# Sixteen experts on one core: conditional rounds for crowded experts replaced by a fixed ninth pass and one conditional block

## The chip, the cores and the metric

The kernel runs on one core of a Trainium2 chip. Its time is the device time of one execution in microseconds (us), and a kernel is told by the median of its runs. The whole network is one program in float32: TensorE multiplies matrices, VectorE and ScalarE do the elementwise work, GpSimd (POOL in the profile) some of it too, and SyncE (SP) issues the loads of weights from HBM into SBUF.

## What is computed

The network has two blocks of two layers each on 256 tokens of 1024 features. The change concerns the second block's feed-forward part, a grouped mixture of experts, which stands in both of its layers:

```python
def grouped_moe(h, router_w, router_b, w_gate, w_up, w_down):
    t = h.reshape(B * S, Dm)                                  # 256 x 1024
    logits = t @ router_w + router_b                          # 16 experts, 4 groups
    probs = softmax(logits)
    group_score = sum of the two best probs of each group
    sel_group = argmax(group_score)
    masked = where(in_group, logits, -inf)
    top_val, top_idx = top_k(masked, 2)
    top_w = softmax(top_val)
    combine = sum(one_hot(top_idx) * top_w)
    for e in range(16):
        hidden = silu(t @ w_gate[e]) * (t @ w_up[e])          # 1024 -> 512
        out = out + combine[:, e:e + 1] * (hidden @ w_down[e])  # 512 -> 1024
    return out
# around it, in each layer i of the block:
h = x * (1.0 + scale) + shift
y = grouped_moe(h, ...)
x = layer_norm_2(ALPHA * x + (1.0 + gate) * y, ln_g[i, 1], ln_b[i, 1])
```

(Cut and slightly abridged; the rest of the network is gated delta rule, dilated and differential attention, dense feed-forward layers, stick-breaking attention and retention.) Each token uses 2 of 16 experts, so an expert has 32 tokens on average, but the inputs decide how many it really has. Each expert has 6 MB of weights: 2 MB each of gate, up and down, 96 MB per layer.

## The kernel before

**Passes.** The router (`router`, up to L1876) gives each token its slot within its experts, the combine weights, and for each of 8 pairs of experts how many more than 64 tokens the fuller one has, in units of 64 (`exi`, L1869 to L1874). `moe` (from L1893) then takes the experts in pairs. Each expert of a pair has 64 slots: the first holds columns 0 to 63 of a tile, the second 64 to 127, and on TensorE their products go into rows 0 to 63 and 64 to 127 of a PSUM bank. A pass of a pair is: **gather** (L1943; VectorE writes a one-hot matrix `pe`, L1953, and TensorE multiplies x with it, L1960, so that `xs` holds the slots' tokens with features on partitions; `pt` is the way back, `cw` the weights), **gate** and **up** (L1982, 32 matmuls each), **flip** (transposes, L1989), **down** (L1996, 32 matmuls), **weigh** (L2001) and **scatter** (L2008, adds the slots to four accumulators in PSUM). The passes overlap: gather and gate of the next pair are written before down of this one, and a pair's scatter after the next gather.

**Conditional rounds.** Behind gate, up and down of each pair stands a nest of three `tc.If(vals[pr] > r)` (`extra_gate` L2016 to L2021, `extra_up` L2029 to L2031, `extra_down` L2041 to L2043). Within it the same pair is done once more for slots 64 to 127, and so on. Each branch is one on every engine, which first loads the condition into a register (L1940).

**Weights.** Pieces of 1 MB are loaded by SP in a fixed order, each into one of three rings, `wq` (8 buffers), `w` (6) and `wr` (NR = 4). `follow` asks for the loads that the pieces just used make room for, behind each branch; loads are not moved across a branch.

**The layer norm's last step.** The gathers of the first two pairs use x before the norm's scale and offset have been applied (they apply them to what they gathered); from pair 2's gather on, x itself must have them. `ln_fix` (L589 to L601) does that on GpSimd, in two halves of 512 columns: it fetches a row of scale and one of offset by DMA (L598), copies them to all partitions (L599) and multiplies and adds (L601). Its rows lie in a tile of its own, `yx`, which has one buffer and is shared with the conditional rounds' `extra_down`. What is traced in Python is scheduled by a framework: it puts instructions on their engines' queues in an order that it works out, gives tiles their buffers, and adds the waits on semaphores.

Of the kernel before, what the change touches and what calls it, by code (L numbers as in the profile page):

```python
# [21 lines left out]
P = 128  # L22
# [93 lines left out]
class Net:  # L116
# [3 lines left out]
    def __init__(self, ctx, tc, T, log=None):  # L120
# [3 lines left out]
        # the sequence of the weights' loads and splits, known from a first trace  # L124
# [3 lines left out]
        self.ltile, self.stile = {}, {}  # L128
# [24 lines left out]
    def segment(self, ny):  # L153
        """The pools of the phases with split weights: the dense ones."""
# [71 lines left out]
    def work(self, items):  # L226
        """A filler out of (ready, generator) items: always the first that is ready."""
# [51 lines left out]
    def ordered(self, *engines):  # L279
        """What is traced within stays in its order on each of these engines."""  # L280
# [13 lines left out]
    def bcast_row(self, pool, src_row, n, tag):  # L294
        """[n] of DRAM -> the same row on all partitions."""
# [7 lines left out]
    def cols(self, pool, src, n, m, tag):  # L303
        """DRAM rows src [n, m, 128] -> tile [128, m, n] (n <= 128, m * n <= 512)."""
# [19 lines left out]
    def wload(self, src, shape, ring="w"):  # L324
        """Ask for one piece of weights, up to 8 KB a partition; wtile gives it."""
# [1567 lines left out]
    def moe(self, layer, xn, out=None):  # L1893
# [11 lines left out]
        with self.wqs, tc.tile_pool(name=self.nm("wr"), bufs=NR) as self.wr, \  # L1905
# [38 lines left out]
            def gather(pr, xs=None, pt=None, cw=None, r=None):  # L1944
# [20 lines left out]
                if pt is None:  # L1965
                    return
# [223 lines left out]
```

## Time and profile before

| | us |
|---|---|
| runs | 2052.61, 2038.22, 2048.41 |
| median | 2048.41 |
| span of the profiled execution | 2037.4 |
| TensorE busy | 1817.7 (89%) |
| VectorE busy | 1052.9 (52%) |
| ScalarE busy | 710.9 (35%) |
| GpSimd busy | 294.6 (14%) |
| bytes loaded | 423.39 MB, mean 208 GB/s |

The profiled execution is told by its span alone: 2037.4 us from its first instruction to its last, 11.0 below the median of the runs and 0.8 below the fastest of them. Busy shares are means over a program of many stages, so a stage is read by itself. In the profile PE is TensorE, PEld its load of the stationary operand, DVE VectorE, ACT ScalarE, POOL GpSimd; a q behind a name means the engine's sequencer, which handles branches, register loads and semaphores. PEclk is the granted share of TensorE's full clock. The line numbers are those of the kernel before.

### The profile page before, as it was taken

The page shows a single profiled execution, that of the slowest core. Times are in us where ns is not written, and L with a number is a line of the kernel's source. Part 1 is how long each engine was busy: PE and PEld are TensorE (multiplying, and loading weights), DVE is VectorE, ACT ScalarE, POOL GpSimd, SP SyncE. Part 2 cuts the span into 40 slices and gives each one's busy share as a digit, 9 for nine tenths or more (in the row PEclk, how much of TensorE's full clock was granted, in tenths as well). Part 3 has the DMA queues.
Part 4 walks back from the last instruction along what each step waited for, and adds up shares of the span by engine and source line. Part 5 has one row for each costly group of instructions (what it writes and reads, how often), then busy time and mean ns, then how long its engine had stood idle before and what let it go on. Part 6 is the DMA issues. An engine that isn't in the chain of part 4 may idle for free. (4 is left out here: it accounts for less than half of the span.)

```text
span 2037.4 us, 29823 instructions
## 1 busy us (share of the span) xinstructions
PE 1817.7 (89%) x11817; PEld 1372.3 (67%) x11817; DVE 1052.9 (52%) x1903; ACT 710.9 (35%) x1339; POOL 294.6 (14%) x293
## 2 busy tenths in 40 slices
PE   7999998999989989999996888997789987788886
PEld 6989877999877779998884343432789864343332
DVE  5766757777567577776654121112756652111213
ACT  5334434555544455555542010110534331110101
POOL 2011104000233130004001100000424301100002
PEclk9999998999889989998997998998899998899998
DMA  8555534555764745566366997673334494899730
GB/s 252 155 166 166 187 126 164 188 186 185 219 198 135 257 157 186 187 206 194 108 217 236 343 394 286 242 269 126 127 124 147 166 370 169 327 337 361 286 141 22
DMA packets 271141, 423.39 MB, mean 208 GB/s; under 512 B 10469, under 2 KB 176951, under 8 KB 270917
## 3 DMA queue, kind: packets, MB, share of 16 engines
q1 hardware_dynamic: 266516, 415.91, 59.1%
q8 instruction: 156, 2.56, 0.5%
q0 software_dynamic: 2016, 2.49, 0.5%
q10 hardware_dynamic: 2385, 1.88, 0.3%
q14 instruction: 68, 0.56, 0.1%
HBM read 419.19 MB, written 1.05 MB: 206 GB/s over the span
## 5 line engine op out<-in xcount | busy, mean ns | idle before, releaser
L268 DVE TENSOR_TENSOR wl<-w,wh 128x1024 fp32r<-128x1024 f32 (+1 forms) x312 | 411.5, 1320 | 217.2 <-ACT wh L267 215.8
L267 ACT ACTIVATE wh<-w 128x1024 fp32r<-128x1024 f32 (+1 forms) x312 | 328.7, 1054 | 369.7 <-PE ps L394 183.9
L393 PE MATMUL ps<-xh,wh 128*128 128x256 f32 (+1 forms) x1312 | 386.6, 295 | 15.3 <-ACT xh L427 8.0
L395 PE MATMUL ps<-xh,wl 128*128 128x256 f32 (+1 forms) x1312 | 378.2, 289 | 5.2 <-DVE wl L268 5.1
L394 PE MATMUL ps<-xl,wh 128*128 128x256 f32 (+1 forms) x1312 | 378.5, 289 | 0.0
L393 PEld LDWEIGHTS ps<-xh,wh 128*128 128x128 f32 (+1 forms) x1312 | 255.7, 195 | 23.2 <-ACT xh L427 8.3
L395 PEld LDWEIGHTS ps<-xh,wl 128*128 128x128 f32 (+1 forms) x1312 | 255.1, 194 | 7.7 <-DVE wl L268 6.1
L394 PEld LDWEIGHTS ps<-xl,wh 128*128 128x128 f32 (+1 forms) x1312 | 255.8, 195 | 3.9 <-issue 1.4
L1982 PE MATMUL pc<-w,xs 128*64 128x512 f32 x512 | 153.3, 657 | 25.0 <-PEq L2043 12.4
L393 PE MATMUL ps<-wh,xh 128*128 128x256 f32 x512 | 155.8, 305 | 5.1 <-DVE rvg L264 2.0
L394 PE MATMUL ps<-wl,xh 128*128 128x256 f32 x512 | 149.0, 291 | 1.1 <-DVE wl L268 1.1
L395 PE MATMUL ps<-wh,xl 128*128 128x256 f32 x512 | 148.6, 291 | 0.2
L394 PE MATMUL pc<-wl,yh 128*128 128x512 f32 x336 | 132.7, 395 | 0.0
L393 PE MATMUL pc<-wh,yh 128*128 128x512 f32 x336 | 131.8, 396 | 0.9 <-DVE yl L268 0.9
L395 PE MATMUL pc<-wh,yl 128*128 128x512 f32 x336 | 131.3, 392 | 1.4 <-DVE yl L268 1.2
L1982 PE MATMUL ps<-w,xs 128*64 128x512 f32 x512 | 120.8, 620 | 0.0
L1982 PEld LDWEIGHTS pc<-w,xs 128*64 128x64 f32 x512 | 44.6, 148 | 109.5 <-issue 100.8
L393 PEld LDWEIGHTS ps<-wh,xh 128*128 128x128 f32 x512 | 101.3, 198 | 10.3 <-issue 2.5
L1960 PEld LDWEIGHTS ps<-pe,x 128*128 128x128 f32 x576 | 73.0, 206 | 46.5 <-issue 45.4
L394 PEld LDWEIGHTS ps<-wl,xh 128*128 128x128 f32 x512 | 101.5, 198 | 1.9 <-DVE wl L268 1.3
L395 PEld LDWEIGHTS ps<-wh,xl 128*128 128x128 f32 x512 | 100.8, 197 | 1.6 <-DVE xl L428 0.7
L1960 PE MATMUL ps<-pe,x 128*128 128x128 f32 x576 | 79.1, 296 | 21.9 <-DVE pe L1953 18.3
(538 smaller groups left out, 2734.1 us busy)
## 6 DMA issues: line engine op xcount, KB each, us to landing
w<-in_moe_w_gate_dram SPq DMA_DIRECT2D x64, 1024.0 KB, 8.7
w<-in_moe_w_up_dram SPq DMA_DIRECT2D x64, 1024.0 KB, 10.7
w<-in_moe_w_down_dram SPq DMA_DIRECT2D x64, 1024.0 KB, 8.6
w<-in_ada_w_dram SPq DMA_DIRECT2D x48, 1024.0 KB, 5.4
w<-in_ffn_w_up_dram SPq DMA_DIRECT2D x44, 1024.0 KB, 5.3
w<-in_ret_w_in_dram SPq DMA_DIRECT2D x24, 1024.0 KB, 5.3
w<-in_ffn_w_down_dram SPq DMA_DIRECT2D x22, 1024.0 KB, 4.9
w<-in_w_in_even_dram SPq DMA_DIRECT2D x21, 1024.0 KB, 5.3
```

The lines of the kernel that those rows point to most:

```text
L267: self.nc.scalar.activation(hi, src, AF.Copy)
L268: self.nc.vector.tensor_tensor(lo, src, hi.bitcast(F32), op=ALU.subtract)
L393: mm(ps, lh, rh, start=first, stop=False)
L394: mm(ps, lh, rl, start=False, stop=False)
L395: mm(ps, ll, rh, start=False, stop=last)
L1960: mm(ps[:, k * P : k * P + P], xn[:, t, (4 * a + k) * P : (4 * a + k + 1) * P], pef[:, t, :], start=t == 0, stop=t == 1)
L1982: mm(ps[64 * e : 64 * e + 64, :], xs[:, k, 64 * e : 64 * e + 64], wt[2 * (k // 4) + e][:, k % 4, :], start=k == 0, stop=k == KD - 1)
```

## The change

The conditional rounds of all pairs go, and with them their branches. In their place comes a ninth pass, `Unit(0)`, which is always done: one expert's slots beyond its first 64, 64 of them. Which expert, and from which slot on, VectorE computes behind the router (`extra_units`, new: some two dozen operations on small tiles) as a mask `m`, an offset `off` and an index `exi`. The pass gathers by mask and offset, and its six pieces of weights are loaded by SP from an address that is computed from a register (`bass.ds(unit_at(u), 1)`). Since one expert alone would fill half of TensorE's rows, its 512 hidden columns are split into two halves of 256 on the two halves of the rows, and in down its 1024 outputs likewise. What one such pass can't take is left to one conditional block, `more(1)`, nested up to the seventh unit, that stands before the last scatter.

Loads are now asked for in one sequence, without `follow`; NR goes from 4 to 6, so the rings have 20 buffers. `ln_fix`'s rows lose `yx` and take a buffer of the tag `xs`, of which there are two and which the gathers use. The last norm's rows (`gb`) move from `xs` into a buffer of the ring. Comments and docstrings were taken out throughout (not shown).

```diff
-NW, NQ, NR = 6, 8, 4
+NX = 7
+NW, NQ, NR = 6, 8, 6
...
+            if src[0] == "dynamic" and src not in self.dyn:
                 break
...
-            self.nc.sync.dma_start(v, bass.AP(tensor=self.byname[name], offset=off, ap=ap))
+            if src[0] == "dynamic":
+                src = self.dyn[src]()
+            else:
+                src = bass.AP(tensor=self.byname[src[0]], offset=src[1], ap=src[2])
+            self.nc.sync.dma_start(v, src)
...
+    def extra_units(self, mp, cnt):
+        nc = self.nc
+        E = N_EXP
+        G = nc.vector
+        tt, ts = G.tensor_tensor, G.tensor_scalar
+        io = self.moe_c[2]["iota64"]
+        tile = lambda n, *s, dt=F32: mp.tile([P, *s], dt, tag="u_" + n, name=self.nm("u" + n), bufs=1)
+        x, y, one = tile("x", E), tile("y", E), tile("one", E)
+        ts(x, cnt, 64.0, None, op0=ALU.is_gt)
+        for r in (2, 3):
+            ts(y, cnt, 64.0 * r, None, op0=ALU.is_gt)
+            tt(x, x, y, op=ALU.add)
+        c = [tile("c0", E), tile("c1", E)]
+        G.tensor_copy(c[0], x)
+        s = 1
+        while s < E:
+            G.tensor_copy(c[1][:, :s], c[0][:, :s])
+            tt(c[1][:, s:], c[0][:, s:], c[0][:, : E - s], op=ALU.add)
+            c.reverse()
+            s *= 2
+        c = c[0]
+        b = lambda v: v[:, None, :].to_broadcast([P, NX, E])
+        iu = io[:, :NX, None].to_broadcast([P, NX, E])
+        m, w = tile("m", NX, E), tile("w", NX, E)
+        tt(m, b(c), iu, op=ALU.is_gt)
+        tt(x, c, x, op=ALU.subtract)
+        tt(w, b(x), iu, op=ALU.is_le)
+        tt(m, m, w, op=ALU.mult)
+        off, ex, exi = tile("off", NX), tile("ex", NX + 1), tile("exi", NX + 1, dt=I32)
+        tt(w, m, b(x), op=ALU.mult)
+        nc.vector.tensor_reduce(off, w, axis=AX.X, op=ALU.add)
+        tt(off, off, io[:, :NX], op=ALU.subtract)
+        ts(off, off, 64.0, -64.0, op0=ALU.mult, op1=ALU.add)
+        tt(w, m, b(io[:, :E]), op=ALU.mult)
+        nc.vector.tensor_reduce(ex[:, :NX], w, axis=AX.X, op=ALU.add)
+        G.tensor_copy(ex[:, NX:], c[:, E - 1 :])
+        G.tensor_copy(exi, ex)
+        return m, off, exi
...
+            def part(u, m, a):
+                d, n = dram[m], (512, 512, 256)[m]
+                v = d[bass.ds(unit_at(u), 1), a * n : a * n + n, :]
+                return v.rearrange("o (k p) f -> p (o k) f", p=P)
...
+                if pr < NP:
+                    src = w[2 * pr + e][:, a * step : a * step + step, :]
+                else:
+                    src = ("dynamic", layer, m, a)
+                    self.dyn[src] = lambda: part(0, m, a)
...
-            slot, comb, exi = self.router(mp, hT)
+            slot, comb, cnt = self.router(mp, hT)
...
-            vals = [nc.values_load(exi[:1, pr : pr + 1], min_val=0, max_val=3) for pr in range(NP)]
...
+            def unit_at(u):
+                if u not in extra:
+                    extra[u] = nc.values_load(extra["exi"][:1, u : u + 1], engines=[mybir.EngineType.SP],
+                                              min_val=0, max_val=N_EXP - 1)
+                return extra[u]
...
+            class Unit(Pair):
...
+                    s.u = u
+                    s.wt = wt or (lambda m: [self.wtile(i) for i in pieces[NP, m]])
+                def slots(s):
+                    m, off = extra["m"], extra["off"]
+                    w = big("uw", [P, 2, NT, N_EXP])
+                    so, cb = big("uso", [P, NT, 2]), big("ucb", [P, NT, 2])
+                    b = m[:, s.u : s.u + 1, :].to_broadcast([P, NT, N_EXP])
+                    tt(w[:, 0], slot, b, op=ALU.mult)
+                    tt(w[:, 1], comb, b, op=ALU.mult)
+                    for i, o in enumerate((so, cb)):
+                        nc.vector.tensor_reduce(o[:, :, 0], w[:, i], axis=AX.X, op=ALU.add)
+                    ts(so[:, :, 0], so[:, :, 0], off[:, s.u : s.u + 1], None, op0=ALU.add)
+                    for o in (so, cb):
+                        nc.vector.tensor_copy(o[:, :, 1], o[:, :, 0])
+                    return gather(so, cb)
+                def up(s, m, xs, ps):
+                    wt = s.wt(m)
+                    for k in range(KD):
+                        for e in range(2):
+                            mm(ps[64 * e : 64 * e + 64, :256], xs[:, k, 64 * e : 64 * e + 64],
+                               wt[k // 4][:, k % 4, 256 * e : 256 * e + 256], start=k == 0, stop=k == KD - 1)
+                    return ps[:, :256]
+                def down(s, hT, cw):
+                    wt = s.wt(2)
+                    y = big("yu", [P, 2, 512], F32R)
+                    ps = self.cb("x")
+                    for f in range(4):
+                        for e in range(2):
+                            c = (f % 2) * P + 64 * (f // 2)
+                            mm(ps[64 * e : 64 * e + 64, :], hT[:, c : c + 64],
+                               wt[f // 2][:, f % 2, e * 512 : e * 512 + 512], start=f == 0, stop=f == 3)
+                    weigh(y, ps, cw)
+                    return y
+                def scatter(s, pt, y, last=False):
+                    for t in range(NT):
+                        for hf in range(2):
+                            sl = slice(64 * hf, 64 * hf + 64)
+                            for v in range(2):
+                                i = mm(acc[t][hf], pt[sl, t * P : t * P + P], y[sl, v, :],
+                                       start=False, stop=last and v == 1)
+                                tc.keep_in_program_order(i)
...
+            def more(u):
+                with tc.If(extra["n"] > u):
+                    wt = {}
+                    for m in range(3):
+                        wt[m] = []
+                        for a in range(2):
+                            k = (4, 4, 2)[m]
+                            if ("w", m, a) not in shared:
+                                ring = self.wr if m < 2 else self.wq
+                                shared["w", m, a] = ring.tile([P, 2048], F32, tag="w", name=self.nm("wx"))
+                            v = shared["w", m, a].rearrange("p (a b) -> p a b", a=k)
+                            nc.sync.dma_start(v, part(u, m, a))
+                            wt[m].append(v)
+                    it = Unit(u, wt.get)
+                    xs, pt, cw = it.slots()
+                    h = gate(it, xs, self.bank())
+                    tt(h, h, it.up(1, xs, self.bank()), op=ALU.mult)
+                    it.scatter(pt, it.down(flip(h), cw))
+                    if u < NX - 1:
+                        more(u + 1)
...
+            its = [Pair(pr) for pr in range(NP)] + [Unit(0)]
+            cur = its[0].slots()
+            h = gate(its[0], cur[0], self.cb("x"))
             back = None
-            for pr in range(NP):
-                last = pr == NP - 1
-                ps = up(pr, 1, xs, self.cb("x") if pr else self.bank(), 0, 4)
-                if pr > 0:
-                    extra_down(pr - 1)
-                up(pr, 1, xs, ps, 4)
+            for n, it in enumerate(its):
+                last = n == NP
+                xs, pt, cw = cur
+                ps = it.up(1, xs, self.cb("x") if n else self.bank())
+                if n == NP - 2:
+                    extra["m"], extra["off"], extra["exi"] = self.extra_units(mp, cnt)
+                    for m in range(3):
+                        for a in range(2):
+                            ask(NP, m, 0, a)
                 tt(h, h, ps, op=ALU.mult)
                 if not last:
-                    nxt = slots(pr + 1)
-                if pr == 0:
+                    cur = its[n + 1].slots()
+                if n == 0:
                     for hf in range(2):
-                        self.ln_fix(big("yx", [P, 2, 512]), xn, 1, layer, 0, hf * 512, 512)
+                        self.ln_fix(big("xs", [P, KD, P], bufs=2).rearrange("p (m a) c -> p m (a c)", m=2),
+                                    xn, 1, layer, 0, hf * 512, 512)
                     fin[:] = scale, shift
-                if pr > 1:
-                    scatter(*back)
-                extra_up(pr)
-                hT = big("hT", [P, 512])
-                flip(h, hT)
+                if n > 0:
+                    back[0].scatter(*back[1:], **({"first": True} if n == 1 else {}))
+                hT = flip(h)
                 if not last:
-                    h = gate(pr + 1, nxt[0])
+                    h = gate(its[n + 1], cur[0], self.bank())
                 else:
                     tail, grow = (self.wq.tile([P, 2048], F32, tag="w", name=self.nm("tail")) for _ in range(2))
                     tail = tail.rearrange("p (t c) -> p t c", t=NT)
                     self.ada_gate_to(grow, ia)
-                y = big("y", [P, 2, 2, 512], F32R)
-                ys = y[:, 0], y[:, 1]
-                pd = down(pr, hT, 0, self.cb("x"))
-                weigh(ys[0], pd, cw)
-                if not last:
-                    extra_gate(pr + 1)
-                pd = down(pr, hT, 1, self.bank())
-                weigh(ys[1], pd, cw)
-                if pr == 0:
-                    scatter(pt, ys, first=True)
-                back = pt, ys
-                if not last:
-                    xs, pt, cw = nxt
+                back = it, pt, it.down(hT, cw)
             if out is not None:
-                gb = [big("xs", [P, D], bufs=2) for _ in range(2)]
+                gb = self.wr.tile([P, 2048], F32, tag="w", name=self.nm("gb")).rearrange("p (m c) -> p m c", m=2)
+                gb = [gb[:, m, :] for m in range(2)]
                 for m in range(2):
                     nc.sync.dma_start(gb[m][:1], T[("ln_g_2", "ln_b_2")[m]][layer, 1:2, :])
                     nc.gpsimd.partition_broadcast(gb[m], gb[m][:1], channels=P)
-            extra_down(NP - 1)
-            scatter(*back, last=True)
+            extra["n"] = nc.values_load(extra["exi"][:1, NX : NX + 1], min_val=0, max_val=NX)
+            shared = {"yu": self.wr.tile([P, 2048], F32, tag="w", name=self.nm("yx"))[:, :1024].bitcast(F32R).rearrange(
+                "p (v c) -> p v c", v=2)}
+            more(1)
+            shared = None
+            back[0].scatter(*back[1:], last=True)
```

How the instructions moved, at the places that matter. On GpSimd (POOL), in layer 0, behind the norm before the experts, the kernel before has this order (`x_81` is x, `yx` the rows' tile, `exi` the rounds' conditions; "waits" lists the semaphores of the engines and DMA queues that a row waits for, ISA without operands prepares the engine for another kind of instruction):

```order
L598 DMA yx_11957<-in_ln_g_dram 1x16x32 [waits DVE_49,DMASW5_49,PE_49,Activation_49]
L598 DMA yx_11957<-in_ln_b_dram 1x16x32 [waits DMASW1_49]
L599 ISA
L599 ISA yx_11957<-yx_11957 128x512 [waits DMASW0_49]
L599 ISA yx_11957<-yx_11957 128x512 [waits DMASW1_49]
L1940 TENSOR_LOAD exi_11550 [waits DMASW5_49,DMASW6_49,DVE_49,DMASW7_49,PE_49,Activation_49]
L2021 COMPARE_AND_BRANCH x3
L2021 UNCONDITIONAL_BRANCH x6
L601 ISA
L601 TENSOR_TENSOR x_81<-x_81,yx_11957 128x2x512 [waits PE_49,Pool_49]
...
L598 DMA yx_11964<-in_ln_g_dram 1x16x32 [waits DMASW2_49,Pool_49]
```

The changed kernel has this there (`xs_11662` and `xs_11669` are the rows' tiles now):

```order
L607 DMA xs_11662<-in_ln_g_dram 1x16x32 [waits DMASW5_49,PE_49,Activation_49]
L607 DMA xs_11662<-in_ln_b_dram 1x16x32 [waits DMASW1_49]
L608 ISA
L608 ISA xs_11662<-xs_11662 128x512 [waits DMASW0_49]
L608 ISA xs_11662<-xs_11662 128x512 [waits DMASW1_49]
L610 ISA
L610 TENSOR_TENSOR x_81<-x_81,xs_11662 128x2x512 [waits PE_49,Pool_49]
L610 TENSOR_TENSOR x_81<-x_81,xs_11662 128x2x512 [waits Pool_49]
L607 DMA xs_11669<-in_ln_g_dram 1x16x32 [waits DMASW2_49,Pool_49]
```

The first fetch of the rows, which had a tile to itself, now takes a buffer of the gathers and waits for TensorE; the second fetch waits for POOL's own work, as before, and the branch between is gone.

On TensorE (PE), at the gather for pair 2 of layer 0, the kernel before has this (`pe` is the one-hot, `pc` and `ps` PSUM banks):

```order
L1982 MATMUL pc_12331<-w_11261,xs_11917 64x512
L1960 MATMUL ps_12480<-pe_12477,x_81 128x128 [waits DVE_49,Activation_49,Pool_49]
L1960 MATMUL ps_12480<-pe_12477,x_81 128x128 [waits DVE_49]
L1960 MATMUL ps_12480<-pe_12477,x_81 128x128 x6
L1960 MATMUL ps_12493<-pe_12477,x_81 128x128 [waits PE_49,Pool_49]
L1960 MATMUL ps_12493<-pe_12477,x_81 128x128 x7
L1969 MATMUL ps_12506<-rcomb_11507,pe_12477 128x16 x2
L1971 MATMUL ps_12506<-ident,pe_12477 128x128 x2
L2031 COMPARE_AND_BRANCH
```

And the changed kernel (L2030 is the gather, L2038 and L2040 its weights and transposes, L2090 a scatter, L2155 a flip, L2069 gate and up, L2080 down):

```order
L2069 MATMUL pc_11726<-w_11261,xs_11622 64x512
L2030 MATMUL ps_11750<-pe_11747,x_81 128x128 [waits Pool_49]
L2030 MATMUL ps_11750<-pe_11747,x_81 128x128 x7
L2030 MATMUL ps_11763<-pe_11747,x_81 128x128 [waits Pool_49]
L2030 MATMUL ps_11763<-pe_11747,x_81 128x128 x7
L2038 MATMUL ps_11776<-rcomb_11497,pe_11747 128x2 [waits DVE_49]
...
L2090 MATMUL pc_11540<-y_11703,pt_11545 128x512 [waits Activation_49]
...
L2155 MATMUL ps_11792<-ident,h_11700 128x128 [waits Activation_49]
...
L2069 MATMUL ps_11799<-w_11263,xs_11744 64x512 [waits DMAHW0_49,Activation_49]
```

Each half of the gather waits for POOL in both. In the change there is no branch behind it, and scatter 0, flip 1 and gate 2 follow it directly.

## Rows read from the trace of the kernel before

**Rows 1.** The page's busy tenths of TensorE, 40 slices of 50.9 us.

```profile
PE   7999998999989989999996888997789987788886
```

**Rows 2.** Table by stage, both layers' experts: us, each engine's busy time (x), PEclk, DMA share, GB/s.

```profile
1096.90:1420.40 323.50, 281.88 (x1293) 123.29 (x1292) 58.76 (x125) 36.59 (x66) 12.22 (x8) 0.95 0.75 275
1696.90:2019.90 323.00, 279.59 (x1293) 123.91 (x1292) 55.64 (x122) 35.76 (x66) 14.67 (x10) 0.96 0.70 256
```

**Rows 3.** TensorE's waits in layer 0's stage: total us, times, longest.

```profile
PE ps L1960 <- DVE pe L1953: 7.9, 4, 4.8
PE ps L1989 <- PEq L2031: 7.1, 4, 3.5
PE pc L1996 <- PEq L2021: 4.9, 3, 1.9
```

**Rows 4.** Timeline of TensorE, layer 0: start us, us, engine line op out<-in, count [idle before <-releaser].

```profile
1099.97 5.76 PE L1982 MATMUL pc<-w,xs 128*64 128x512 f32 x25 [1.15 <-PEq L2021]
...
1112.96 3.84 PE L1960 MATMUL ps<-pe,x 128*128 128x128 f32 x32
...
1117.00 0.41 PE L1971 MATMUL ps<-ident,pe 128*128 128x128 f32 x2
1120.47 0.63 PE L1989 MATMUL ps<-ident,h 128*128 128x128 f32 x4 [3.06 <-DVEq L2031]
1121.03 8.78 PE L1982 MATMUL ps<-w,xs 128*64 128x512 f32 x32
...
1185.58 2.09 PE L2008 MATMUL pc<-y,pt 128*128 128x512 f32 x8
```

**Rows 5.** The extra round of layer 0 on TensorE, and all matmuls on xo (ns min/median/max).

```profile
1277.92 3.81 PE L1960 MATMUL ps<-pe,x 128*128 128x128 f32 x32 [1.38 <-DVE pe L1953]
...
1283.23 7.09 PE L1982 MATMUL ps<-w,xo 128*64 128x512 f32 x32 [0.89 <-ACT po L262]
...
1341.58 6.47 PE L1996 MATMUL ps<-w,ho 128*64 128x512 f32 x25
...
L1982 PE MATMUL ps<-w,xo x128: 592/592/643, 1283.2 to 1960.7; 128*64 128x512 f32 x128
```

**Rows 6.** Timeline of VectorE behind the router, layer 0.

```profile
1094.49 0.41 DVE L439 TENSOR_SCALAR xs<-ps,lnada 128x128 f32<-128x128 f32 x1 [3.38 <-PE ps L1960]
```

**Rows 7.** Timeline of POOL, layer 0, then layer 1.

```profile
1077.90 0.49 POOL L598 DMA_DIRECT2D yx<-in_ln_b_dram  x1
1084.74 1.48 POOL L599 PARTITION_BROADCAST yx<-yx  x2 [6.35 <-DVE rlg L1773]
...
1120.24 0.71 POOL L598 DMA_DIRECT2D yx<-in_ln_g_dram  x1 [0.29 <-POOL x L601]
...
1131.80 1.48 POOL L599 PARTITION_BROADCAST yx<-yx  x2 [10.35 <-PE pc L1996]
1143.57 4.92 POOL L601 TENSOR_TENSOR x<-x,yx 128x1024 f32<-128x1024 f32 x2 [10.29 <-issue]
...
1720.57 0.71 POOL L598 DMA_DIRECT2D yx<-in_ln_g_dram  x1 [0.29 <-POOL x L601]
...
1745.93 4.76 POOL L601 TENSOR_TENSOR x<-x,yx 128x1024 f32<-128x1024 f32 x2 [12.49 <-issue]
```

**Rows 8.** Two stretches of layer 0, columns as in rows 2.

```profile
1120.00:1135.00 15.00, 13.05 (x52) 4.51 (x54) 1.59 (x4) 0.60 (x1) 2.68 (x4) 0.89 0.82 292
...
1185.00:1200.00 15.00, 13.21 (x64) 5.75 (x65) 2.85 (x7) 1.82 (x4) 0.00 (x0) 1.00 1.04 390
```

**Rows 9.** The page's DMA issues: count, KB each, median us from issue to landing.

```profile
w<-in_moe_w_up_dram SPq DMA_DIRECT2D x64, 1024.0 KB, 10.7
```

**Rows 10.** Timeline of TensorE at the end of layer 0's stage.

```profile
1408.37 1.95 PE L1501 MATMUL ps<-ident,adac 128*128 128x128 f32 x16
...
1415.94 1.45 PE L1996 MATMUL ps<-w,hT 128*64 128x512 f32 x5
...
1418.95 1.42 PE L2008 MATMUL pc<-y,pt 128*128 128x512 f32 x5 [0.17 <-DVEq L2043]
```

More of the change, by code (lines that the diff above doesn't have):

```diff
@@ L328, in wload @@
         if self.rec:
-            self.loads.append((src.tensor.name, src.offset, [list(a) for a in src.ap], shape, ring))
+            at = src if isinstance(src, tuple) else (src.tensor.name, src.offset, [list(a) for a in src.ap])
+            self.loads.append((at, shape, ring))
         if self.rec:
@@ L337, in _loads_to @@
         while self.lnext <= min(i, len(self.loads) - 1):
-            name, off, ap, shape, ring = self.loads[self.lnext]
+            src, shape, ring = self.loads[self.lnext]
             if ring == "wq" and self.wq is None or ring == "wr" and self.wr is None:
+                break
+            if src[0] == "dynamic" and src not in self.dyn:
                 break
@@ L1873, in router @@
-        tt(ex8[:, 0, :], ex8[:, 0, :], ex8[:, 2, :], op=ALU.add)
-        nc.vector.tensor_copy(exi, ex8[:, 0, :])
-        return slot, comb, exi
+        cnt = mp.tile([P, E], F32, name=self.nm("cnt"), bufs=1, tag="r_cnt")
+        nc.vector.tensor_copy(cnt, ps[:, 2 * E : 3 * E])
+        return slot, comb, cnt
+    def extra_units(self, mp, cnt):
[36 more added lines that the diff above has]
+        return m, off, exi
@@ L1900, in moe @@
         cst = self.moe_c[2]
-        wg = T["moe_w_gate_2"][layer].rearrange("e (k p) f -> e p k f", p=P)
-        wu = T["moe_w_up_2"][layer].rearrange("e (k p) f -> e p k f", p=P)
-        wd = T["moe_w_down_2"][layer].rearrange("e (k p) d -> e p k d", p=P)
+        dram = [T[f"moe_w_{n}_2"][layer] for n in ("gate", "up", "down")]
+        wg, wu, wd = (w.rearrange("e (k p) f -> e p k f", p=P) for w in dram)
         NP = N_EXP // 2
@@ L1913, in moe, with big @@
             for pr, m in order:
-                step, w = (4, 4, 2)[m], (wg, wu, wd)[m]
                 for a in range(2):
                     for e in range(2):
-                        i = self.wload(w[2 * pr + e][:, a * step : a * step + step, :], [P, step, w.shape[3]],
-                                       ring=("wq" if nload % NB < NQ else "w" if nload % NB < NQ + NW else "wr"))
-                        pieces.setdefault((pr, m), []).append(i)
-                        nload += 1
-            end = pieces[NP - 1, 2][-1]
-            self._loads_to(pieces[0, 0][0] + NB - 1)
-            follow = lambda pr, m: self._loads_to(min(pieces[pr, m][-1] + NB, end + NW - 1))
-            big = lambda tag, shape, dt=F32, bufs=1: mp.tile(shape, dt, tag=tag, name=self.nm(tag), bufs=bufs)
+                        ask(pr, m, e, a)
+            shared = None
+            def big(tag, shape, dt=F32, bufs=1):
+                if shared is not None and tag in shared:
+                    return shared[tag]
+                t = mp.tile(shape, dt, tag=tag, name=self.nm(tag), bufs=bufs)
+                if shared is not None:
+                    shared[tag] = t
+                return t
             hT = big("y", [P, KD, S])
@@ L1955, in gather @@
                 pef = pe.rearrange("p t e s -> p t (e s)")
-                for a in range(2 if xs is not None else 0):
+                for a in range(2):
                     ps = self.bank()
@@ L1973, in gather @@
                     sl = slice(64 * e, 64 * e + 64)
[L1974 removed]
+                    ts(cw[sl], ps[sl, 256 + e : 257 + e], 0.5, None, op0=ALU.mult)
                 self.copy(pt, ps[:, :S])
[L1977 to L1998 removed]
+                return xs, pt, cw
             def weigh(y, pd, cw):
@@ L2002, in weigh @@
                 stt(y[:, 1, :], pd, cw, y[:, 0, :].bitcast(F32), op0=ALU.mult, op1=ALU.subtract)
-            def scatter(pt, ys, hfs=(0, 1), first=False, last=False):
-                for t in range(NT):
-                    for hf, y in zip(hfs, ys):
-                        for v in range(2):
-                            i = mm(acc[t][hf], pt[:, t * P : t * P + P], y[:, v, :],
-                                   start=first and v == 0, stop=last and v == 1)
-                            tc.keep_in_program_order(i)
@@ L2063, in gate, with flip @@
+            def gate(it, xs, ps):
+                ps = it.up(0, xs, ps)
+                h = big("h", [P, 512])[:, : it.n]
                 self.silu2(h, ps, h)
                 return h
-            xs, pt, cw = slots(0)
-            h = gate(0, xs)
-            extra_gate(0)
-            back = None
-            for pr in range(NP):
-                last = pr == NP - 1
-                ps = up(pr, 1, xs, self.cb("x") if pr else self.bank(), 0, 4)
-                if pr > 0:
-                    extra_down(pr - 1)
-                up(pr, 1, xs, ps, 4)
+            def flip(h):
+                n = h.shape[1]
+                ps = self.bank()
+                for f in range(n // P):
+                    nc.tensor.transpose(ps[:, f * P : f * P + P], h[:, f * P : f * P + P], self.ident)
+                hT = big("hT", [P, 512])[:, :n]
+                self.copy(hT, ps[:, :n])
+                return hT
```

131 lines of the change are left out of this document (52 added, 79 removed).

## The prediction, made before the changed kernel ran

> **What bounds the kernel now.** I began with the page's busy tenths [rows 1]: TensorE is the busiest engine nearly everywhere, but in the stretch from the 22nd slice (layer 0's experts) and again from the 34th (layer 1's) it falls to 7 and 8. The change touches these two stretches alone; on every engine the order of all other work is what it was. So I next took the table by stage, from the first expert matmul to the end of the last scatter [rows 2]: 323.5 and 323.0 us, with TensorE busy for 281.9 and 279.6 of them and the DMA engines for 0.75 and 0.70. Neither bounds the stage alone: some 41 us per layer are holes on TensorE, and the weights have slack on average.
>
> The view of waits shows where the holes are [rows 3]: most releasers are a sequencer at a conditional branch (L2021, L2031, L2043), or VectorE's one-hot for an extra round (L1953). TensorE's timeline gives the price of each piece of work between them [rows 4]: a gather takes 1112.96 to 1117.41 = 4.45 us, a flip 0.63, a scatter 2.1; 32 expert matmuls (a gate, an up or a down) take 7.09 [rows 5]. A hole also costs clock: behind 3.06 us of idling the same 32 matmuls took 8.78 us instead of 7.09 (+1.7). One pair without holes is then 4.45 + 3 x 7.09 + 0.6 + 2.1 = 28.4 us; I use 28.8, since a change of line loses a tenth or two.
>
> The extra round [rows 5]: xo's 128 matmuls are 2 x (32 gate + 32 up), so exactly one round runs in each layer. Gather and gate take 1277.92 to 1290.3 = 12.4; up and flip at the prices above 7.7; down (its greater part at 1341.58) and scatter 9.2: about 30 us with a little idling.
>
> **Part by part.** *Removed:* the round, 30 us, and the branches with their holes, most of 41 us, in each layer.
>
> *Added, ninth pass:* its matmuls are 256 wide in gate and up (half of 7.09 each: 3.6) and 8 instead of 16 in each half's down (3.6); with gather 4.45, flip 0.3 and scatter 2.1 it is some 18 us. Its small VectorE operations (about 22) follow the router's, which start 0.10 to 0.12 us apart there; VectorE then idles 3.38 us anyway [rows 6], so they can delay the first pass by 0 to 1.5; I take 0.5, since most fit into that hole.
>
> *Moved, and this is the large new cost:* the rows of layer-norm scale and offset lose their own tile (yx) and share xs with the gathers. Before, the first half's rows were fetched and broadcast ahead of the experts, at 1077.9 and 1084.74 [rows 7], so only the second half's chain ran beside them: issue 1120.24, broadcast 1131.80, multiply and add 1143.57 to 1148.49, in all 28.3 us (layer 1: 1720.57 to 1750.7, 30.1). After, the first fetch must wait until the up pass of pair 0 has read xs, and the second fetch waits for the first multiply. Both chains stand in line, 2 x 29.2 = 58.5 us, from 15.0 us on (gate and up of pair 0, 1097 to 1113 less the branch's 1.15). In the changed order TensorE's gather for pair 2 waits for POOL, half by half, and scatter 0, flip 1, gate 2 and down 1 are queued behind it. Without waiting, TensorE gets there at 15.0 + 4.45 + 0.6 + 3 x 7.0 = 41.1; its second half may start at 73.5. So about 30 us of the holes return as a single one, in each layer.
>
> *Ring of 20 buffers instead of 18, asks no longer tied to branches:* a saturated stretch moved 390 GB/s [rows 8], 2.7 us a 1 MB piece (I take 2.75); a pair needs 12 in 28.8 us, 2.4 each. The loads lose 12 x 2.75 - 28.8 = 4.2 us, 1.5 pieces, per pair, some 10 by the end; the hole of 30 us refills the ring. I cost this at nothing; what hides it is that hole. Without it, 102 pieces at 2.75 = 280 us less 16 to 20 already there would come close to binding a stage of 250.
>
> *Addresses from registers:* the six loads stand at the end of SP's queue, about 45 us ahead of use (19 pieces at 2.4). Landing takes 10.7 us for a piece of an up matrix [rows 9]; I take the same, the upper end is rival 4. Layer 1 loads the register earlier in SP's queue; its value has long been there, so nothing is held up.
>
> *Tail:* the last conditional stands between the ninth down and the last scatter. The present tail has one too: last down ends at 1417.4, the scatter resumes at 1418.95 behind 0.17 us of VectorE's branch [rows 10]. I take weighing 1.5, branch 2 (0 to 5, the upper end from the holes of 3 to 3.5 at branches in rows 3), scatter 2.1: 5.6.
>
> **The sum, per layer.** 73.5 to the second half of gather 2; rest of it 2.8, lost clock 1.8 (as in rows 4), scatter 0, flip 1, gate 2, down 1 together 16.7: 94.8. Pairs 2 to 6, 5 x 28.8 = 144.0: 238.8. Up 7, gather 9, scatter 6, flip, half gate, down 7: 24.8, gives 263.6. Up 9 3.6, scatter 7 2.1, flip 0.3, the adaLN gate's transposes 1.95, down 9 3.6, and 0.9 between them: 12.5, gives 276.1. Tail 5.6, start 0.5: **282.2 against 323.5 and 323.0**, 41 less in each layer, 82 in all. The profiled span is 2037.4; it becomes 1955. That execution lies 11 us below the median of the runs (2048.41), so by the median I forecast **1966**. Its own terms (POOL's idle 10.3 to 12.5 each, start, branch, clock) give -5 to +10 a layer: 1956 to 1986.
>
> **Rivals.**
> 1. *The chain hides nothing and holds nothing up*: the fetch doesn't wait, by the framework's placing of buffers. TensorE saves those 30 us and the clock's 1.8 too: 1966 - 64 = 1902, held back by the loads to about 1918. Against it: the order shows the waits on POOL. Chance 0.06.
> 2. *POOL changes over faster.* It idles 10.3 to 12.5 us ahead of a broadcast and of a multiply in the experts' stretch, but only 6.35 from the end of the issue in the first one (1078.4 to 1084.74) [rows 7]. At 6.35 for all four, a chain is 1.2 + 6.35 + 1.5 + 6.35 + 4.9 = 20.3, two 40.6, gather 2's second half starts at 55.6: 18 us less a layer, 1930. Chance 0.12. [...] I take the longer ones since they stand beside the experts' loads, as both new chains will.
> 3. *POOL slower still*: with the DMA engines busy without a break, each change takes some 4 us more (the broadcast at 1131.80 had a DMA share of 0.82 beside it, where 1.04 is to be had [rows 8]): four changes, 17 us a layer: 2000. Chance 0.11.
> 4. *Slower than before:* the register-addressed loads. If a load of this kind held SP's queue for its full landing, 6 x 10.7 = 64 us against 45 of lead would make the ninth pass 19 us late, 2004. From (45 + 41 + 10) / 6 = 16 us a load on, the kernel is over 1% slower; at 20 us it is 6 x 20 - 45 = 75 a layer, 2116. No row of before shows such a load; the nearest (rows 9) lies well below 16. Chance 0.04.
> 5. *The change doesn't do what it says*: the conditional block is entered since one ninth pass isn't enough. It loads six pieces (10.7 + 5 x 2.75 = 24) and then computes 18 to 21 us: 45 in a layer, 2011. Rows 5 show one round a layer, which speaks against, though a round served both experts of a pair; the reference's routing of these inputs has one expert above 64 tokens in each layer. Chance 0.03.
>
> My forecast keeps 0.64.
>
> **How the numbers follow.** The range 1925 to 2003 takes in the forecast, rivals 2 and 3 and their bounds: it leaves out rival 1, the far end of 4 and 5, some 0.15. 1% (20 us) is what a measurement of this kernel can tell from no change: faster than 2028 are all but the worse half of rival 4 and several delays at once. Faster 0.92, same 0.04, slower 0.04.
>
> **What would show it.** In the changed trace: (a) stages of about 282 us; (b) one hole of about 30 us on TensorE in front of the gather's second half, released by POOL, some 50 to 75 us after the first expert matmul; before it two fetch, broadcast, multiply chains on POOL of 29 us each; (c) no holes at branches until the tail, and no wait for weights later than the hole; (d) the ninth pass's matmuls about 18 us, its loads landing before use; (e) no matmuls of the conditional block. Wrong would be the forecast if gather 2 isn't late (rival 1), if POOL's idle is near 6 or above 14 (2, 3), or if TensorE waits for the six loads (4).

## The result, and the profile after

The changed kernel takes **1948.27 us** (median of 4 runs, 1945.98 to 1951.72) against 2043.32 (4 runs, 2033.93 to 2052.61) beside it: a ratio of 0.9537, 95% interval 0.9498 to 0.9575, 95 us less. Forecast were 82 less (1966, range 1925 to 2003). The profiled execution's span went from 2037.4 to 1950.0 us, 87 less.

The busy tenths of TensorE, to be laid beside [rows 1]:

```profile
PE   7999998999989989999999759999679997879995
```

Within the stages one short dip is left in each (the 5 in the 24th slice, of 48.75 us, and the 8 and 7 in the 35th and 36th); the 6 and 7 in the 29th and 30th lie between the stages. The table by stage, from the first expert matmul to the end of the last scatter, columns as in [rows 2]:

```profile
1099.08:1376.20 277.12, 252.70 (x1275) 118.00 (x1274) 52.01 (x118) 37.66 (x71) 14.73 (x12) 0.96 0.88 334
1656.64:1930.00 273.36, 247.98 (x1275) 117.40 (x1274) 51.24 (x114) 36.41 (x71) 17.21 (x14) 0.96 0.82 316
```

The stages fell by 46.4 and 49.6 us; the sum said 282.2 for each. (Outside them this one execution is 8.6 us longer, and nothing here explains it by the change: the kernel before and its variant with another constant, below, do the same work up to the first expert matmul and reach it at 1096.90 and 1103.96 us.) TensorE's waits in layer 0's stage, all over 0.5 us, beside [rows 3]:

```profile
PE ps L2030 <- POOL x L610: 20.3, 1, 20.3
PE ps L2155 <- DVE h L2195: 1.6, 2, 0.8
PE pc L2141 <- PEq L2162: 0.8, 1, 0.8
PE pc L2080 <- DVE hT L266: 0.8, 1, 0.8
```

One hole is left, at the gather for pair 2, and the releaser is POOL's `ln_fix`, as forecast; the branch at the end (L2162) costs 0.8, and no wait is on weights. POOL's timeline in layer 0, beside [rows 7]:

```profile
1113.62 0.71 POOL L607 DMA_DIRECT2D xs<-in_ln_g_dram  x1 [35.06 <-issue]
...
1123.26 1.48 POOL L608 PARTITION_BROADCAST xs<-xs  x2 [8.43 <-issue]
1133.95 4.78 POOL L610 TENSOR_TENSOR x<-x,xs 128x1024 f32<-128x1024 f32 x2 [9.21 <-issue]
1139.03 0.71 POOL L607 DMA_DIRECT2D xs<-in_ln_g_dram  x1 [0.29 <-POOL x L610]
...
1147.46 1.48 POOL L608 PARTITION_BROADCAST xs<-xs  x2 [7.21 <-issue]
1156.57 4.75 POOL L610 TENSOR_TENSOR x<-x,xs 128x1024 f32<-128x1024 f32 x2 [7.64 <-issue]
```

The first fetch waits until pair 0's up has read xs, and two chains follow in line, 1113.62 to 1161.32: 47.7 us, not 58.5, since POOL idles 7.2 to 9.2 before each operation instead of 10.3 to 12.5. TensorE on either side of the hole, and in a pair much later:

```profile
1139.07 2.05 PE L2030 MATMUL ps<-pe,x 128*128 128x128 f32 x16
1161.37 3.78 PE L2030 MATMUL ps<-pe,x 128*128 128x128 f32 x16 [20.25 <-POOL x L610]
...
1195.29 0.60 PE L2155 MATMUL ps<-ident,h 128*128 128x128 f32 x4
...
1202.74 3.60 PE L2080 MATMUL pc<-w,hT 128*64 128x512 f32 x16
1206.17 3.60 PE L2080 MATMUL ps<-w,hT 128*64 128x512 f32 x16
...
1222.74 0.60 PE L2155 MATMUL ps<-ident,h 128*128 128x128 f32 x4
...
1288.12 1.02 PE L2080 MATMUL pc<-w,hT 128*64 128x512 f32 x2
1288.97 1.02 PE L2080 MATMUL ps<-w,hT 128*64 128x512 f32 x2
1289.93 1.83 PE L2030 MATMUL ps<-pe,x 128*128 128x128 f32 x14
1291.68 1.50 PE L2080 MATMUL pc<-w,hT 128*64 128x512 f32 x5
...
1295.26 1.60 PE L2030 MATMUL ps<-pe,x 128*128 128x128 f32 x12
1296.80 1.07 PE L2080 MATMUL pc<-w,hT 128*64 128x512 f32 x2
...
1298.66 0.94 PE L2030 MATMUL ps<-pe,x 128*128 128x128 f32 x6
...
1300.14 1.50 PE L2080 MATMUL pc<-w,hT 128*64 128x512 f32 x5
...
1303.72 1.35 PE L2090 MATMUL pc<-y,pt 128*128 128x512 f32 x3
...
1315.22 0.66 PE L2155 MATMUL ps<-ident,h 128*128 128x128 f32 x4 [0.78 <-DVE h L2195]
...
1349.84 0.66 PE L2155 MATMUL ps<-ident,h 128*128 128x128 f32 x4 [0.78 <-DVE h L2195]
```

From flip to flip a pair takes 1222.74 - 1195.29 = 27.45 us early, but 1349.84 - 1315.22 = 34.6 late, with under 1 us of idling in it. In gate, up and down each expert of a pair has one half of TensorE's 128 columns (`128*64` in the rows), and in the written order the two experts' matmuls come in turns. In the late pairs the scheduler has put pieces of down between pieces of the next gather, which uses all the columns (`128*128`). Down's records then come two of one PSUM bank and two of the other, by their pace all of one expert, and then the gather's: four records take 1.81 us (1288.12 to 1289.93) where sixteen in turns took 3.43. The four pieces of this down take 1.81 + 3.58 + 1.86 + 3.58 = 10.8 us; the early one takes 6.9. This is not in the prediction.

### The profile page after: what moved, and what is told of

Read it like the earlier page. It is cut to its first block, busy times and chain, and to the rows that moved or that the text cites. A ratio compares the mean times of both kernels' runs of the same rounds, so it can differ in the third digit from the quotient of the medians.

```text
span 1950.0 us, 29353 instructions
## 1 busy us (share of the span) xinstructions
PE 1756.9 (90%) x11781; PEld 1359.4 (70%) x11781; DVE 1042.3 (53%) x1941; ACT 712.6 (37%) x1349; POOL 292.5 (15%) x293
## 5 line engine op out<-in xcount | busy, mean ns | idle before, releaser
L270 DVE TENSOR_TENSOR wl<-w,wh 128x1024 fp32r<-128x1024 f32 (+1 forms) x312 | 405.4, 1300 | 225.0 <-ACT wh L269 223.8
L2069 PE MATMUL pc<-w,xs 128*64 128x512 f32 x512 | 119.8, 594 | 0.0
L2030 PEld LDWEIGHTS ps<-pe,x 128*128 128x128 f32 x576 | 73.9, 209 | 65.4 <-POOL x L610 43.0
L2030 PE MATMUL ps<-pe,x 128*128 128x128 f32 x576 | 80.0, 299 | 43.0 <-POOL x L610 41.0
L2069 PE MATMUL ps<-w,xs 128*64 128x512 f32 x512 | 113.3, 595 | 0.9 <-ACT pt L264 0.9
L446 ACT ACTIVATE xs<-ps,adac 128x128 f32<-128x128 f32 x56 | 25.6, 457 | 178.8 <-DVE xs L448 178.8
```

Of the source, the lines that this page charges most:

```text
L270: self.nc.vector.tensor_tensor(lo, src, hi.bitcast(F32), op=ALU.subtract)
L446: self.nc.scalar.activation(out, in_, AF.Identity, scale=a, bias=b)
L2030: mm(ps[:, k * P : k * P + P], xn[:, t, (4 * a + k) * P : (4 * a + k + 1) * P], pef[:, t, :], start=t == 0, stop=t == 1)
L2069: mm(ps[64 * e : 64 * e + 64, :], xs[:, k, 64 * e : 64 * e + 64], wt[2 * (k // 4) + e][:, k % 4, :], start=k == 0, stop=k == KD - 1)
```

## The experiments

Each time is the median of 4 runs. The kernel before was timed beside each: 2036.7 beside own rows, written order, both edits and no ninth pass; 2041.8 beside down apart and the two variants of the kernel before; 2040.5 beside fixed addresses and no block. Differences of a few us between runs of different groups are within that.

**Own rows.** The shared tile undone:

```diff
-NW, NQ, NR = 6, 8, 6
+NW, NQ, NR = 6, 8, 5
-  self.ln_fix(big("xs", [P, KD, P], bufs=2).rearrange(...), xn, ...)
+  self.ln_fix(big("yx", [P, 2, 512], bufs=2), xn, ...)
-  gb = self.wr.tile([P, 2048], ...)
+  gb = [big("yx", [P, 2, 512], bufs=2)... for _ in range(2)]
```

> The changed kernel, but the rows of ln_fix have two buffers of their own again (yx, 8 KB), so both halves' rows are fetched and broadcast ahead of the experts and POOL only multiplies and adds beside them; for room NR is 5 instead of 6 (19 ring buffers), and the last norm's rows share yx. Theory A (the shared tile makes the hole of 20.3 and 20.8 us at pair 2's second half of the gather): the hole is gone, its slow-clock matmuls too (1.5 us), some 22 us less a layer. The scheduler's order of the last pairs changes with it: one more pair of each layer has its matmuls mixed with others', and pairs so mixed took 34.6 us instead of 27.45 in the changed kernel, so 5 to 8 us a layer come back: 28 to 40 us less in all, a time of about 1912 (1905 to 1922). Rival B (the hole only stands where the ring would run dry anyway, so that without it TensorE waits for weights): under 10 us less, 1938 or above, with waits of TensorE on weights in pairs 3 to 7.

Measured 1926.17, ratio 0.9436 (0.9400 to 0.9472): 22 us less than the changed kernel, above theory A's range and below rival B's 1938. Its trace tells why. The timeline of POOL:

```profile
1080.35 0.71 POOL L607 DMA_DIRECT2D yx<-in_ln_g_dram  x1 [1.14 <-ACT x L699]
...
1089.28 2.86 POOL L608 PARTITION_BROADCAST yx<-yx  x4 [6.77 <-issue]
1116.36 9.61 POOL L610 TENSOR_TENSOR x<-x,yx 128x1024 f32<-128x1024 f32 x4 [24.21 <-PE ps L2030]
```

The hole is gone (POOL ends at 1126, TensorE needs x some 15 us later), and no wait on weights took its place, so rival B falls. But the stage fell only from 277.1 to 264.7: the scheduler, its hole gone, mixes one pair more, and the flips of four late pairs lie 33.4 to 34.6 us apart. I had allowed 5 to 8 us a layer for that; in layer 0 it was about 10 (the excess over 27.45 adds up to 27 us there, against 17 in the changed kernel).

**Written order.** TensorE keeps the order of the program within the experts:

```diff
+  keep = self.ordered(nc.tensor.engine)
+  keep.__enter__()
   cur = its[0].slots()
...
+  keep.__exit__(None, None, None)
   extra["n"] = nc.values_load(...)
```

> The changed kernel with one edit: within the experts TensorE keeps the order in which the passes are written, so no pass's matmuls are mixed with another's. Theory C (matmuls of a pair's two experts, on two halves of the columns, run beside each other only when they alternate; the mixed order of the last pairs breaks that, 34.6 us a pair instead of 27.45): pairs 4 to 7 of layer 0 and 6 to 7 of layer 1 go back to 27.5 us, 17 and 12 us less, and 1 to 2 us at the ninth pass: 28 to 34 us less in all, 1917 (1911 to 1924). Rival D (the last pairs are slow since their weights come late, and the mixing only fills that time): no change or slower, 1945 to 1955, with waits on weights. The hole of 20 us on POOL stays by both.

Measured 1916.92, ratio 0.9401 (0.9375 to 0.9427): 31 us less, as theory C said. POOL's hole stands, and a late pair of layer 0 takes 1330.20 - 1302.76 = 27.4 us from flip to flip, as an early one does:

```profile
PE ps L2030 <- POOL x L610: 19.9, 1, 19.9
```

```profile
1302.76 0.60 PE L2155 MATMUL ps<-ident,h 128*128 128x128 f32 x4
...
1330.20 0.60 PE L2155 MATMUL ps<-ident,h 128*128 128x128 f32 x4
```

Order alone costs the changed kernel those 31 us, and TensorE waits for no weights in this stage; rival D falls.

**Down apart.** On top of the written order, the two experts' blocks one after the other within down:

```diff
-  for f in range(4):
-      for e in range(2):
+  for e in range(2):
+      for f in range(4):
           mm(ps[64 * e : 64 * e + 64, :], hT[...], wt[2 * (f // 2) + e][...], ...)
```

> The changed kernel with TensorE in the written order (1917), but in down the four blocks of the first expert are written ahead of those of the second, instead of in turns; the same matmuls on the same operands. Theory C (matmuls on the two halves of the columns run side by side only when they alternate): each down takes some 13.5 us instead of 6.9, in 8 pairs of 2 layers: 105 us more, about 2022 (2000 to 2030), as the other instructions stay. The hole on POOL comes later by nothing, and the slower pace gives the weights more slack. Rival D (order within a pass means nothing): 1917, within 5.

Measured 1936.16, ratio 0.9476 (0.9442 to 0.9510): 19 us more than the written order, neither 105 nor none. In the traces the two stages are 12.8 and 13.8 us longer, and a pair takes 29.3 us from flip to flip instead of 27.45. A down of this kernel on TensorE:

```profile
1194.00 4.08 PE L2080 MATMUL pc<-w,hT 128*64 128x512 f32 x13
1197.49 0.64 PE L2080 MATMUL ps<-w,hT 128*64 128x512 f32 x1
1197.91 0.59 PE L2080 MATMUL pc<-w,hT 128*64 128x512 f32 x1
1197.97 0.59 PE L2080 MATMUL ps<-w,hT 128*64 128x512 f32 x1
```

Starts 0.06 us apart (1197.91 and 1197.97) are read as two records on the two halves of the columns, beside each other; of one stream a record comes every 0.43 (1197.91, 1198.34, 1198.77). The second half here starts before the first half's records are through: thirteen take 4.08 us, not 13 x 0.43 = 5.6. So records need not alternate strictly; theory C was too strong: blocks of eight records cost 1.9 us a pair, the mixed order of the changed kernel 7.2. Of these 7.2 down takes 4.0 (10.8 instead of 6.9); the rest is up and scatter, which are mixed too, and 0.8 of idling. That a piece of one expert has nothing to run beside when matmuls over all the columns part it from the other's is read from these paces; no run put such matmuls between the two experts alone.

**Both edits together.**

> Both edits together: own rows for ln_fix, loaded ahead (NR 5), and TensorE in the written order. Theories A and C: the hole's 20.3 and 20.8 us with 1.5 us of clock each, and the mixed pairs' 30 us, so some 74 us less than the changed kernel: 1874. Each stage is then about 238 us, in which 82 pieces have to come behind the first 20 at 2.62 us each (400 GB/s), 215 us: the weights are nearly the bound, which may give back up to 10 us: 1872 to 1886. Rivals B and D: weights bind in earnest, over 15 us of waits on them in each layer, 1905 or more.

Measured **1881.51**, ratio 0.9238 (0.9212 to 0.9264): 67 us below the changed kernel, within the range given for A and C. It beats both kernels. Layer 0's stage takes 241.8 us; the weights now begin to bind, by 2.2 us here and 3.3 in layer 1:

```profile
1305.47 1.95 PE L2120 MATMUL ps<-w,xs 128*64 128x256 f32 x16 [1.52 <-DMA w<-in_moe_w_gate_dram]
1308.08 1.95 PE L2120 MATMUL ps<-w,xs 128*64 128x256 f32 x16 [0.67 <-DMA w<-in_moe_w_gate_dram]
```

**Without the ninth pass.** `its` ends with the eight pairs, and the addresses and the block are left out.

> The changed kernel without the ninth pass, its addresses and the conditional block (so slots beyond 64 of an expert are not computed). The prediction costs the pass at some 18 us of TensorE and the tail's branch at 2: 20 us a layer, 40 in all; the scheduler also mixes fewer pairs here (about one and a half instead of three), which gives 7 to 10 us a layer more: about 55 less, 1893 (1885 to 1905). If the ninth pass's register-addressed loads or the branch cost more than that, the time falls below 1880.

Measured 1893.64, ratio 0.9285 (0.9254 to 0.9315): 54.6 us less, as expected: 27 a layer for the pass, its tail and the mixing it brings.

**Fixed addresses.**

```diff
-  v = d[bass.ds(unit_at(u), 1), ...]
+  v = d[bass.ds(unit_at(u), 1) if u else slice((10, 13)[layer], (11, 14)[layer]), ...]
```

> The changed kernel, but the ninth pass loads its weights from fixed addresses (expert 10 in layer 0, 13 in layer 1, those that the registers name on these inputs) instead of from a register. By my prediction the address costs nothing, since the six loads are issued well ahead: 1948, within 5. By rival 4 (register-addressed loads hold SP's queue) the changed kernel would lose time here: 10 us or more less, under 1938.

Measured 1947.95, ratio 0.9541 (0.9512 to 0.9570): the same as the changed kernel's 1948.27. So these loads cost it nothing by their address, and the prediction's rival 4 falls.

**Without the block**, in the kernel with both edits.

> Own rows and written order together (1881.5), without the conditional block at the end (enough for these inputs, where one ninth pass takes all that is over). The block's branch shows as 4.2 and 1.3 us of TensorE's sequencer ahead of the last scatter, some of it beside the weighing (1.5) that stays, and the slow clock behind it 0.8: 1 to 4 us a layer, so 1876 (1872 to 1880). Rival: a block that isn't entered costs more than its branch, by keeping the next phase's loads and VectorE's work behind it: 10 us or more less, under 1871.

Measured 1880.83, ratio 0.9212 (0.9184 to 0.9239): 0.7 us less than with it, no difference that the times can tell, and just above the range. The traces do tell one: the branch's wait ahead of the last scatter (4.2 and 1.3 us) is gone, and the stages are 3.1 and 0.6 us shorter (238.7 against 241.8 in layer 0). So in these two executions a block that isn't entered costs some 4 us in both layers together, which the expectation allowed for and which is no more than the runs of one kernel spread; the rival falls.

**The kernel before, no round taken.** The counts are compared with a million:

```diff
-  ts(ex8[:, r, :], cnt, 64.0 * (r + 1), None, op0=ALU.is_gt)
+  ts(ex8[:, r, :], cnt, 1e6 * (r + 1), None, op0=ALU.is_gt)
```

> The kernel before with its counts compared with a million instead of 64, so that every branch stands and is asked, but no extra round runs (slots beyond 64 of an expert are not computed). The prediction's price of the two rounds, 30 us each: 60 us less than before, about 1977 (1967 to 1987). Rival: the rounds fill time in which the weights or a branch would be waited for anyway; then under 40 us less, 1997 or more.

Measured 1988.00, ratio 0.9736 (0.9702 to 0.9770): 54 us less than the kernel before, 27 a round, just above the range. The price of 30 was slightly high.

**The kernel before, no branches.** `extra_gate`, `extra_up` and `extra_down` give way to their `follow`:

```diff
-  extra_up(pr)
+  follow(pr, 1)
```

> The kernel before without the conditional rounds and their branches; the loads are still asked for at the same places. By the prediction's 41 us of holes per layer at branches and extra rounds, some 8 of which went with the round: 33 us a layer below the run whose branches are never taken, less a hole of 7 that POOL's one chain then makes, so about 1925. By comparison with the changed kernel without ninth pass (1894, with a hole of 20 to 21 us a layer in place of 7): about 1870. If it is near 1925 the branches cost their visible holes; near 1870 they cost 20 us a layer more, in broken order, late asks for weights and lost clock.

Measured 1880.42, ratio 0.9202 (0.9174 to 0.9229): **108 us less than with branches that are never taken**, 54 a layer. Layer 0's stage, first with branches never taken, then without, columns as in [rows 2]:

```profile
1103.96:1400.12 296.16, 253.77 (x1147) 110.73 (x1146) 52.34 (x112) 31.90 (x57) 12.23 (x8) 0.94 0.82 300
```

```profile
1102.62:1343.30 240.68, 235.97 (x1147) 104.12 (x1146) 50.23 (x106) 34.59 (x64) 12.10 (x8) 1.00 0.97 367
```

The stage is 55.5 us shorter for the same 1147 matmuls: idling is 42.4 against 4.7, and the busy time itself 17.8 less. Some 15 of these 17.8 are the slow clock behind holes (a mean of 0.94 against 1.00, and 0.06 of 253.8 is 15: an estimate); the rest goes with the order of the matmuls, which changes too. With branches, two of TensorE's waits, and the branches' records of one line on two engines' sequencers (PEld's is TensorE's; ns min/median/max):

```profile
PE ps L1989 <- PEq L2031: 7.3, 4, 3.5
PE ps L1960 <- DVE pe L1953: 7.3, 3, 4.9
```

```profile
L2021 PEldq COMPARE_BRANCH x16: 427/5973/6377, 1103.5 to 1930.7; - x16
L2021 DVEq COMPARE_BRANCH x16: 56/56/72, 1105.3 to 1935.7; - x16
```

These branches, never taken, lasted 0.4 to 6.4 us each on TensorE's sequencer and under 0.1 on VectorE's. What the DMA queues of instructions moved within the stage, first with branches, then without (packets, MB, share):

```profile
q8 instruction: 42, 0.69, 0.9%
q14 instruction: 16, 0.13, 0.1%
```

```profile
q8 instruction: 9, 0.15, 0.3%
q14 instruction: 3, 0.02, 0.0%
```

With branches the two queues moved 58 packets in the same work, without them 12, and TensorE had holes of up to 3.5 us at the branches. That the holes wait for these packets is not shown: branches and packets went together. The run also takes out, with the branches, the limits that they set to the order of instructions; the two were not parted.

## Why the prediction was right, and where its terms were off

**What held.** The parts of the working are the right ones: the rounds and the branches' holes go, the ninth pass comes in, and gather 2 waits for POOL behind two chains that stand in line. Rivals 1, 4 and 5 didn't happen: the loads come in time with a register's address, and the conditional block isn't entered. The account by runs is: 54 us out with the rounds, 108 with the branches, 55 in with the ninth pass and block, and some 13 in from the rest (the changed kernel without ninth pass, 1893.6, less the kernel before without branches, 1880.4). That the four come to 94 out, beside a measured 95, is no check of them: they are the steps of one chain of runs from the kernel before to the changed one. The 13 are a balance: from flip 0 to flip 1, where the hole lies, the first of these two kernels takes 20.6 and 20.4 us more in the two layers, and in the pairs behind it, of which it mixes fewer, 8 and 13 less.

**Terms of the sum in layer 0.** From the stage's start to the second half of gather 2: forecast 73.5, measured 1161.4 - 1099.1 = 62.3. Pairs 2 to 6, from flip 2 to flip 7: forecast 144.0, measured 1349.84 - 1195.29 = 154.6. The rest of the stage is some 4 us shorter than forecast. Two errors of 11 us stood against each other, which was luck; the stage of 277 beside a forecast of 282 looks better than its parts.

*Step: "That execution lies 11 us below the median of the runs".* By the span the forecast was 1955, and 1950.0 was measured; by the median it was 1966, and 1948.27 was measured. The changed kernel's profiled execution lies 1.7 us above its median, so that 13 of the 18 us by which the forecast was high are this term. It was the spread of three runs, and a fourth brought the median of the kernel before to 2043.32. The other 5 are luck again: the two stages came out 14 us shorter than forecast together, and the rest of this execution 8.6 longer.

*Step: "POOL's idle 10.3 to 12.5 each".* I took [rows 7] because they "stand beside the experts' loads, as both new chains will". They also stood beside branches, and the changed kernel has none. The second chain in the kernel before with branches never taken, and then without branches:

```profile
1138.64 1.48 POOL L599 PARTITION_BROADCAST yx<-yx  x2 [10.02 <-issue]
1149.78 4.93 POOL L601 TENSOR_TENSOR x<-x,yx 128x1024 f32<-128x1024 f32 x2 [9.66 <-issue]
```

```profile
1131.41 1.48 POOL L599 PARTITION_BROADCAST yx<-yx  x2 [6.40 <-issue]
1140.74 4.78 POOL L601 TENSOR_TENSOR x<-x,yx 128x1024 f32<-128x1024 f32 x2 [7.85 <-issue]
```

Same tiles, same order on POOL but for the branches: 10 us against 6.4 and 7.9. (The idle ahead of a broadcast also holds the rows' way from HBM: the second row landed 5.6 us after its issue with branches and 4.8 without, which is 0.8 of the 3.6 between them.) So rival 2 was half of the truth, and rival 3 the wrong way round: the changed kernel's chains ran beside a DMA share of 1.02 to 1.06 and were shorter (47.7 us for both in layer 0 instead of 58.5). The idle was 6.40 and 7.85 in this chain without branches, 7.1 to 9.2 in the changed kernel, 9.7 and 10.0 beside branches that are never taken, and 10.2 to 12.5 in the kernel before. What sets its length was not isolated.

*Step: "One pair without holes is then 28.4 us; I use 28.8".* The true pace is 27.45 in written order and up to 34.6 in mixed order. The mixing could be read in the order of the changed kernel's instructions before it ran; I looked there for waits alone and not for what stands between two experts' matmuls.

*Step: "some 41 us per layer are holes".* As a price of the branches it was low by 13 us a layer (54): the clock behind a hole was lower too (0.89 in the 15 us behind the one of 3.06 [rows 4], 1.00 from 1185 to 1200 [rows 8]), and [rows 3] count waits alone. Nor did the round take holes with it: TensorE idles 42.4 us in layer 0's stage without the round and 41.6 with it [rows 2]. The working read VectorE's one-hot (L1953) as that of an extra round; it is that of every gather, and only one of those four waits, 1.38 us [rows 5], was the round's. The sum didn't need this term, since it was built up from the pieces of the new stage; that is why the forecast stood.

## What to carry to other kernels

Price the new stage from its own pieces, not the old one less what is removed: the branches showed as 41 us of waits a layer and took 54 in the time. When an edit saves memory by sharing a tile, ask which early load now waits for the tile's reader: here 4 KB of rows (a partition) made a hole of 20 us a layer, while POOL, whose load it was, had been idle for 35 us. And where matmuls of two independent halves run side by side, read in the instruction order whether they stay neighbours; here a scheduler that parted them took 34.6 us a pair instead of 27.45, with under 1 us of idling a pair to show for it.

## What was not expected of the hardware

In the experts' stage POOL idled ahead of a broadcast or a multiplication of the rows' chain for 7.1 to 9.2 us in the changed kernel and for 6.4 and 7.9 in the kernel before without branches, but for 10.2 to 12.5 in the kernel before and for 9.7 and 10.0 in it with branches never taken. Down's records (`128*64`, 512 wide) came every 0.45 us where one expert's stood by themselves (four in 1.81 us) and every 0.21 with the two experts' in turns (sixteen in 3.43); with the halves written one after the other thirteen took 4.08 us, which lies between the two paces.
